# Running sums of the forget gate in four one-pass products, and eight transfers moved from SyncE to GpSimd

## Chip, core and metric

The kernel runs on one core of one Trainium2 chip. The metric is the device time of one execution in microseconds (us). Before the change the median of three runs is 347.56 us (347.39 to 348.7).

## What is computed

One decoder block over 256 tokens (`S`) of width 1024 (`D`), in float32. The reference, cut to what matters here:

```python
h = rms_norm(x, attn_norm_g)
proj = h @ w_in              # qa, ka, va, qb, kb, vb, f_logit, g_logit
...                          # branch a: attention over qa, ka, va with rotary embedding
log_f = log_sigmoid(f_logit + b_forget)          # 8 heads
c = cumsum(log_f, axis=-1)                       # branch b, the forgetting attention
s = (qb . kb) * scale + c[t] - c[s]              # causal, then softmax, then times vb
gates = sigmoid(g_logit + b_gate)                # 2 branches x 1024
merged = gates[0] * (o_a @ w_branch_moba) + gates[1] * (o_b @ w_branch_fox)
x = x + merged @ w_out
h2 = rms_norm(x, ffn_norm_g)
u, g = split(h2 @ w_ffn_up)                      # 2 x 2816
x = x + (silu(causal_conv3(g)) * u) @ w_ffn_down
```

## The kernel before

Every large product is made of float32r products, which TensorE takes in one pass. Each operand is split into a high part (the value written as float32r) and a low part (the rest), and three products are added in PSUM: high times high, high times low, low times high. Small products stay in plain float32: the transposes, the products of the forget gate and some of the scores.

The weights come in chunks of 128 x 2048 float32 (1 MB). SyncE issues them in order through `load` (L131) into three buffers `raw`. For each half of a chunk ScalarE writes the high part `whi` (L134) and VectorE the low part `wlo` (L135). `use` takes a half and loads ahead by five halves (`AHEAD`). The first chunk of weights comes together with x, transposed, in eight transfers of 384 KB (`lead`, L95). `split_x` (L162, L164, L165) makes the high and low parts of x times the norm's gain, and L102 and L103 split the weights beside it.

TensorE's order is written out by hand in the text of the kernel. The other engines and the DMA issues are ordered by a scheduler at build time, which places an instruction where it finds the engine free and the operands and buffers ready. An instruction can so stand far ahead of its place in the text. An engine then works off its own list strictly in order.

The stages, in TensorE's order: nine warm-up products on a constant (L171); the projections qa, ka, va, qb, kb (`project`, L247); the running sums (`forget_c`, L364); three pairs of heads of branch a's scores (`scores`, L400, L407); vb and the gate projections (`gate`, L247) with the rest of the attention between them (L413, L450, L464); the branch products (L604); the output projection and the up projection (`rows_of`, L653, L654) with the down projection (L792) in between; the final sums and stores (L815, L816, L825, L826).

What the change touches:

- `forget_a` to `forget_c`: the logits are made in `forget_products` (L326), turned to tokens by heads in `forget_b`, and sent through the log-sigmoid in small VectorE and ScalarE steps that end in `lf`, 128 x 16 (L356). In `forget_c` two plain float32 products (L364), one per half of the tokens, multiply `lf` with the triangle `tri` (128 x 128, a slice of the constants `cst`). VectorE copies the sums to SBUF (L366) and adds the first half's last column to the second half (L367), ScalarE's queue writes them to DRAM (L369) and reads them back spread over 128 partitions (L370). They are used in the scores of branch b.
- `norm1`: the sum of squares (L222 transposes, L224 sums) and the inverse root (L200 to L205).
- `ones`, a 128 x 128 block of ones as float32r (L638), used in `norm2_sum` (L719).
- `gate_bias` (L477): two calls, two transfers of 256 KB in each, g = 0 and 1 and later g = 2 and 3, into the two buffers `lows`. The third waits until `gate` has used the first (L490), the fourth until it has used the second. They are consumed by L490.
- `start_turn` (L298): turns of the queries and keys by 16 small transfers each, half of them issued by GpSimd and half by SyncE; `end_turn` (L304) copies them out on ScalarE, and for branch b `halve` (L392, L393) splits them.
- `spread_x` (L738): 16 transfers of 64 KB that lay the residual out for the final sums. GpSimd issues 11 and SyncE five. They wait for `turn_x` (L733), and are read at L805 and L815.

Of the kernel before, what the change touches and what calls it, by code (L numbers as in the profile page):

```python
# [8 lines left out]
F32 = mybir.dt.float32  # L9
F32R = mybir.dt.float32r  # L10
BF16 = mybir.dt.bfloat16
AF = mybir.ActivationFunctionType
ALU = mybir.AluOpType
# [4 lines left out]
P = 128  # L18
S = 256
NT = 2  # L20
# [3 lines left out]
NH = 8  # L24
# [18 lines left out]
def decoder_block(ctx, tc, a, out):  # L43
    nc = tc.nc
# [6 lines left out]
    def T(shape, tag, bufs=1, dt=F32):  # L51
        return sb.tile(shape, dt, tag=tag, bufs=bufs, name=tag)

    def bank():
        return ps.tile([P, 512], F32, tag="bank", bufs=8, name="bank")
# [97 lines left out]
    def col(c, n=1):  # L153
        return sm[:, c:c + n]
# [32 lines left out]
    cst = T([P, 832], "cst")  # L187
    nc.sync.dma_start(cst, a["consts"])
    ident = cst[:, 0:128]
    tri = cst[:, 128:256]  # L190
    mask3 = cst[:, 384:768]
    cos2 = cst[:, 768:832].rearrange("p (t c) -> p t c", t=NT)
    wfr = T([P, KT, NH], "wfr")
# [2 lines left out]
    def rsqrt_mean(dst, ss, n, shape, tag, bufs=2):  # L196

        w = T([P, 3] + shape, tag, bufs)
        v, y, t = w[:, 0], w[:, 1], w[:, 2]
        nc.vector.tensor_scalar(v, ss, 1.0 / n, EPS, op0=ALU.mult, op1=ALU.add)  # L200
        nc.scalar.activation(t, v, AF.Ln)
        nc.scalar.activation(y, t, AF.Exp, scale=-0.5)
        nc.vector.scalar_tensor_tensor(t, v, -0.5, y, op0=ALU.mult, op1=ALU.mult)
        nc.vector.tensor_tensor(t, t, y, op=ALU.mult)
        nc.vector.scalar_tensor_tensor(dst, t, 1.5, y, op0=ALU.add, op1=ALU.mult)  # L205
# [13 lines left out]
    def norm1():  # L219
        ssp = bank()  # L220
        for t in range(NT):
            nc.tensor.transpose(ssp[:, t * P:(t + 1) * P], xss[:, 0, t * P:(t + 1) * P], ident)  # L222
        ss = T([P, NT], "ss1")
        nc.vector.tensor_reduce(ss, ssp[:, 0:S].rearrange("p (t c) -> p t c", t=NT), axis=AX.X, op=ALU.add)  # L224
        rsqrt_mean(rs, ss, D, [NT], "rsv")

        for i in range(2):
            gr = sm[:, C_GR + 16 * i:C_GR + 16 * (i + 1)][:, None, :].to_broadcast([P, NT, 16])
            rc = T([P, NT, 16], f"rc{i}")
            rsn = T([P, NT, 16], f"rsn{i}")  # L230
            nc.vector.tensor_tensor(rc, cos2[:, :, 0:16], gr, op=ALU.mult)
            nc.vector.tensor_tensor(rsn, cos2[:, :, 16:32], gr, op=ALU.mult)
            rope.append((rc, rsn))
# [76 lines left out]
    bias = T([P, NH, 384], "bias")  # L310

    fg = {}

    def forget_a():
        wf4 = T([P, KT, 32], "wf4")
        nc.gpsimd.memset(wf4, 0.0)
        nc.gpsimd.tensor_tensor(wf4[:, :, 0:8], wfr, g1[:, :, None].to_broadcast([P, KT, NH]), op=ALU.mult)
        fg["wf4"] = wf4
# [12 lines left out]
    def forget_b():  # L331
        fs = fg["fs"]
        ft = bank()
        for t in range(NT):
            nc.tensor.transpose(ft[:, t * P:(t + 1) * P], fs[:, t * P:(t + 1) * P], ident)
        z = T([P, NT, NH], "z")
        nc.vector.tensor_reduce(z, ft[:, 0:S].rearrange("p (t g e) -> p t g e", t=NT, e=32)[:, :, :, 0:NH].rearrange("p t g h -> p t h g"), axis=AX.X, op=ALU.add)
        for t in range(NT):
            nc.vector.scalar_tensor_tensor(z[:, t], z[:, t], rs[:, t:t + 1], col(C_BF, NH), op0=ALU.mult, op1=ALU.add)

        az = T([P, NT, NH], "az")
        nc.scalar.activation(az, z, AF.Abs)
        e = T([P, NT, NH], "ez")
        nc.scalar.activation(e, az, AF.Exp, scale=-1.0)
        u = T([P, NT, NH], "uz")
        nc.vector.tensor_scalar_add(u, e, 1.0)
        l = T([P, NT, NH], "lz")
        nc.scalar.activation(l, u, AF.Ln)
        d = T([P, NT, NH], "dz")
        nc.vector.scalar_tensor_tensor(d, u, -1.0, e, op0=ALU.add, op1=ALU.subtract)  # L350
        r = T([P, NT, NH], "rz")
        nc.vector.reciprocal(r, u)
        nc.vector.tensor_tensor(d, d, r, op=ALU.mult)
        nc.vector.tensor_tensor(l, l, d, op=ALU.subtract)
        lf = T([P, NT, NH], "lf")
        nc.vector.scalar_tensor_tensor(lf, z, 0.0, l, op0=ALU.min, op1=ALU.subtract)  # L356
        fg["lf"] = lf

    def forget_c():
        lf = fg["lf"]  # L360
        cp = bank()
        c0, c1 = (cp[:NH, t * P:(t + 1) * P] for t in range(NT))
        for t, c in enumerate((c0, c1)):
            nc.tensor.matmul(c, lf[:, t], tri, start=True, stop=True)  # L364
        cT = T([P, 2, 384], "pT", 4)[:NH, 0, 0:S]
        nc.vector.tensor_copy(cT, cp[:NH, 0:S])  # L366
        nc.vector.tensor_scalar_add(cT[:, P:S], cT[:, P:S], cT[:, P - 1:P])  # L367
        cd = dr.tile([NH, S], F32, name="cd")
        nc.scalar.dma_start(cd, cT)  # L369
        nc.scalar.dma_start(bias[:, :, P:P + S], bass.AP(tensor=cd.tensor, offset=cd.offset, ap=[[0, P], [S, NH], [1, S]]))  # L370
# [101 lines left out]
    bg = []  # L472

    def gate_bias():
        for g in range(len(bg), len(bg) + 2):
            bg.append(T([P, 2, S], "lows", 2).rearrange("p j t -> p (j t)"))
            nc.sync.dma_start(bg[g], a["bg"][:, g])  # L477

    def gate(c, late=False):
        g, h = divmod(c, 2)  # L480
# [23 lines left out]
    project(0, pq, 1)  # L504
    project(1, pk, 0)
    norm1()
    forget_products()
    q0 = start_turn(finish_qk(pq, 0, 0), 0)
# [6 lines left out]
    project(3, pq, 0)  # L515
    project(3, pq, 1, (0,))
    forget_b()
    project(3, pq, 1, (1,))
    q1 = finish_qk(pq, 1, 0)
    pk = banks()  # L520
    project(4, pk, 0)
    gate_bias()
    end_turn(q0, 0, 0)
    end_turn(k0, 0, 1)
    project(4, pk, 1, (0,))
    state["hold"] = True
    project(4, pk, 1, (1,))
    forget_c()
    scores(0, 0)
    state["hold"], state["behind"] = False, (None, last_max[0])  # L530
# [38 lines left out]
    values(0, (0, 1))  # L569
    values(0, (2, 3))  # L570
    gate_bias()
    for c in (4, 5, 6):
        gate(c)
# [60 lines left out]
    hx = T([P, KT, 2, 2, P], "pp", 1, F32R)  # L634
    acc = [[None, None] for _ in range(NT)]
    rs2 = T([P, S], "rsB")
    ones = T([P, P], "ones", 1, F32R)
    nc.scalar.activation(ones, cst[:, 256:384], AF.Copy)  # L638

    def place(t, dh):  # L640
# [88 lines left out]
    x1 = lt[:, :, S:2 * S]  # L729
    turned_x = lt[:, :, 2 * S:3 * S]  # L730
# [4 lines left out]
    def spread_x():  # L735
        for r in range(4):
            for b in range(4):
                (nc.sync if b == 3 or r == b == 0 else nc.gpsimd).dma_start(x1[32 * b:32 * (b + 1), r::4], turned_x[32 * r:32 * (r + 1), b::4])  # L738


    acts = {}
# [94 lines left out]
    for f in range(NF):  # L836
        low = up_finish(f, first[f] if f < 2 else up_products(f))
        if f % 2 == 0 and f >= 4:
            down(f // 2 - 2)
        if TURN <= f < TURN + KT:  # L840
            turn_x(f - TURN, low)
        if f == TURN + KT:
            spread_x()
# [73 lines left out]
```

## Time and profile before

| | before |
|---|---|
| median of 3 runs (range) | 347.56 us (347.39 to 348.7) |
| the profiled execution's own time | 347.68 us |
| its span, first to last instruction | 345.9 us |
| TensorE (PE) busy | 341.7 us |
| VectorE (DVE) busy | 296.4 us |
| ScalarE (ACT) busy | 220.5 us |
| GpSimd (POOL) busy | 24.2 us |
| read from and written to HBM | 67.64 MB and 1.06 MB |

The profiled execution lies 0.12 us above the median of the runs, and its time 1.78 us above its span. The parts of a profile used here: the busy times of the engines; the waits, which name for an engine's idle time what ended it; the chain of work that ended last, followed back from the last instruction; the timeline, which lists instructions by start time with neighbours of one kind merged (start, us from the first start to the last end, engine, line, operation, output and inputs, count); and windows, which give busy time by stretch of the span with the DMA engines' mean busy share and rate. PE is the matrix product, PEld the loading of its stationary operand, SPq, ACTq and POOLq are the sequencers that issue transfers.

### The profile page before, as it was taken

What the parts mean: (1) busy time and instruction counts of PE and PEld (TensorE: products, weight loads), DVE (VectorE), ACT (ScalarE), POOL (GpSimd) and SP (SyncE); (2) the same over time, 40 slices, a digit from 0 to 9 for tenths busy, and PEclk for the clock granted to TensorE, in tenths of its full rate; (3) what the DMA queues carried; (4) which work ended last, traced back from release to release, by engine and by line L of the source; (5) the groups of instructions that cost most, each with busy time, mean ns of one, the idle gap of its engine ahead of it and who ended that gap; (6) DMA issues with size and microseconds to landing.
All of it is one profiled execution on the core that took longest, in us unless ns stands there. A gap on an engine that the chain in (4) does not pass through costs nothing.

```text
span 345.9 us, 5459 instructions
## 1 busy us (share of the span) xinstructions
PE 341.7 (99%) x1983; PEld 299.9 (87%) x1983; DVE 296.4 (86%) x562; ACT 220.5 (64%) x384; POOL 24.2 (7%) x51
## 2 busy tenths in 40 slices
PE   9999999999999999999999999999999999999996
PEld 5888888888888888889999998989898999989885
DVE  4899997999989578997999998897859898968853
ACT  4968556877599485745767876664645674756430
POOL 0000261044000000000000000000000000060000
PEclk9999999999999999999999999999999999999999
DMA  7987859667941827484726645664573565594003
GB/s 268 409 345 261 305 173 308 243 181 216 353 166 36 331 85 245 158 312 173 244 81 284 208 169 233 243 244 142 222 244 121 200 214 196 186 282 142 2 0 121
DMA packets 17466, 72.19 MB, mean 209 GB/s; under 512 B 2856, under 2 KB 7408, under 8 KB 10016
## 3 DMA queue, kind: packets, MB, share of 16 engines
q1 hardware_dynamic: 14864, 69.02, 55.8%
q0 software_dynamic: 1376, 1.77, 2.1%
q10 hardware_dynamic: 1200, 1.06, 0.9%
q8 instruction: 15, 0.25, 0.3%
q14 instruction: 11, 0.09, 0.1%
HBM read 67.64 MB, written 1.06 MB: 199 GB/s over the span
## 4 chain that ended last, share of the span: by engine, by line
PE 99%; DVE 0%; issue 0%
PE bank L247 30%; PE bank L653 26%; PE bank L792 17%; PE bank L654 13%; PE bank L604 6%; PE bank L464 2%; PE bank L171 1%; PE bank L450 1%; PE bank L400 1%; PE bank L407 1%; PE bank L413 0%; PE bank L618 0%; PE bank L326 0%; PE bank L364 0%; DVE s L825 0%; PE bank L719 0%
## 5 line engine op out<-in xcount | busy, mean ns | idle before, releaser
L135 DVE TENSOR_TENSOR wlo<-raw,whi 128x1024 fp32r<-128x1024 f32 x94 | 113.8, 1218 | 5.5 <-ACT whi L134 5.2
L134 ACT ACTIVATE whi<-raw 128x1024 fp32r<-128x1024 f32 x94 | 97.9, 1052 | 18.4 <-PE bank L247 5.9
L247 PE MATMUL bank<-whi,x 128*128 128x512 f32 x320 | 84.3, 383 | 0.1
L653 PE MATMUL bank<-pp,whi 128*128 128x512 f32 x232 | 76.6, 382 | 0.0
L247 PEld LDWEIGHTS bank<-whi,x 128*128 128x128 f32 x320 | 60.3, 190 | 10.8 <-ACT whi L102 1.2
L654 PE MATMUL bank<-pp,wlo 128*128 128x256 f32 x232 | 63.2, 273 | 0.0
L653 PEld LDWEIGHTS bank<-pp,whi 128*128 128x128 f32 x232 | 43.8, 189 | 6.1
L247 PE MATMUL bank<-wlo,x 128*128 128x512 f32 x160 | 47.6, 379 | 0.0
L654 PEld LDWEIGHTS bank<-pp,wlo 128*128 128x128 f32 x232 | 44.5, 192 | 0.2
L247 PEld LDWEIGHTS bank<-wlo,x 128*128 128x128 f32 x160 | 30.2, 189 | 4.3
L792 PE MATMUL bank<-whi,qT 128*128 128x512 f32 (+1 forms) x92 | 27.8, 370 | 0.0
L761 DVE TENSOR_TENSOR sq<-bank,lows 128x256 f32<-128x256 f32 x44 | 18.2, 416 | 8.7 <-ACT lows L760 8.6
L766 ACT ACTIVATE s<-sq,sm 128x256 f32<-128x256 f32 x22 | 13.1, 598 | 18.8 <-DVE sq L762 18.8
L738 POOL DMA_DIRECT2D lead<-lead x11 | 5.8, 536 | 219.4 <-DVE lead L733 219.3
L298 POOL DMA_DIRECT2D pp<-pp x32 | 17.1, 542 | 46.8 <-DVE qf L268 22.1
L769 ACT ACTIVATE s<-s 128x256 f32<-128x256 f32 x22 | 9.1, 415 | 16.4 <-DVE s L768 16.4
L792 PEld LDWEIGHTS bank<-whi,qT 128*128 128x128 f32 x92 | 17.2, 189 | 2.3
L653 PE MATMUL bank<-pp,bias 128*128 128x512 f32 x56 | 18.7, 382 | 0.0
L760 ACT ACTIVATE lows<-bank 128x256 f32<-128x256 f32 x44 | 15.8, 369 | 2.8 <-PE bank L654 2.7
L792 PE MATMUL bank<-wlo,qT 128*128 128x512 f32 (+1 forms) x46 | 17.0, 370 | 0.0
L604 PE MATMUL bank<-whi,pp 128*128 128x512 f32 x64 | 16.9, 382 | 0.0
L431 ACT ACTIVATE s<-s,nm 128x128 f32<-128x128 f32 (+1 forms) x32 | 14.1, 448 | 2.8 <-DVE nm L428 2.8
(181 smaller groups left out, 592.2 us busy)
## 6 DMA issues: line engine op xcount, KB each, us to landing
raw<-in_wu SPq DMA_DIRECT2D x22, 1024.0 KB, 4.9
raw<-in_wd SPq DMA_DIRECT2D x11, 1024.0 KB, 4.9
raw<-in_qkv SPq DMA_DIRECT2D x9, 1024.0 KB, 5.5
raw<-in_wg SPq DMA_DIRECT2D x8, 1024.0 KB, 5.5
raw<-in_wb SPq DMA_DIRECT2D x4, 1024.0 KB, 4.9
raw<-in_wo SPq DMA_DIRECT2D x4, 1024.0 KB, 4.7
lead<-in_lead SPq DMA_DIRECT2D x8, 384.0 KB, 6.5
raw<-in_qkv SPq DMA_DIRECT2D x2, 512.0 KB, 8.4
```

The lines of the kernel that those rows point to most:

```text
L134: whi = nc.scalar.activation(hi, raw, AF.Copy)
L135: wlo = nc.vector.tensor_tensor(lo, raw, hi.bitcast(F32), op=ALU.subtract)
L247: nc.tensor.matmul(pt[t], lhs[:, k, t * P:(t + 1) * P], rhs, start=(k == 0 and i == 0), stop=(k == KT - 1 and i == 2))
L298: queues[r % len(queues)].dma_start(raw[32 * r:32 * (r + 1), :, b], y[32 * b:32 * (b + 1), r])
L431: last_exp[:] = [nc.scalar.activation(s[:, j, c], s[:, j, c], AF.Exp, scale=-1.0, bias=nm[:, j, i:i + 1], accum_out=l[:, j, i:i + 1])]
L604: nc.tensor.matmul(ps_[t], lhs[:, t * P:(t + 1) * P], rhs, start=(k == 0 and i == 0), stop=(k == 3 and i == 2))
L653: nc.tensor.matmul(two[i], wh[:, c], both, start=(k == 0), stop=False)
L654: nc.tensor.matmul(two[i][:, 0:S], wl[:, c], high, start=False, stop=(k == KT - 1))
L760: nc.scalar.activation(lows[:, i:i + 1].rearrange("p b (a t) -> p b a t", a=2), apart(two[i][:, S:2 * S], 1), AF.Copy)
L761: nc.vector.tensor_tensor(halves(ev[:, i:i + 1]), apart(two[i][:, 0:S], 1), halves(lows[:, i:i + 1]), op=ALU.add)
L766: nc.scalar.activation(cv, g, AF.Identity, scale=col(C_CW + 2 * NF + f), bias=col(C_CB + f))
L792: nc.tensor.matmul(o, lhs, rhs, start=(first and i == 0), stop=(end and i == 2))
```

## The change

The log gates `lf` are copied to a high part as float32r and the rest is kept as a low part, both in a new tile `lf2`. The triangle is converted once to a float32r tile `tri` by ScalarE in `norm1`, written between L224 and the inverse root. In `forget_c` four float32r products (two parts, two halves of the tokens) take the place of two float32 products. `ones` takes over the buffer of `tri`. Of the four transfers of `gate_bias`, all but the first are issued by GpSimd, and all 16 of `spread_x` are.

```diff
-    tri = cst[:, 128:256]
...
         nc.vector.tensor_reduce(ss, ssp[:, 0:S].rearrange("p (t c) -> p t c", t=NT), axis=AX.X, op=ALU.add)
+        nc.scalar.activation(tri, cst[:, 128:256], AF.Copy)
         rsqrt_mean(rs, ss, D, [NT], "rsv")
...
     fg = {}
+    tri = T([P, P], "tri", 1, F32R)
...
         nc.vector.scalar_tensor_tensor(lf, z, 0.0, l, op0=ALU.min, op1=ALU.subtract)
-        fg["lf"] = lf
+        lf2 = T([P, 4, NT, NH], "lf2", 1, F32R)
+        nc.vector.tensor_copy(lf2[:, 0], lf)
+        nc.vector.tensor_tensor(lf2[:, 1], lf, lf2[:, 0].bitcast(F32), op=ALU.subtract)
+        fg["lf"] = lf2
...
         for t, c in enumerate((c0, c1)):
-            nc.tensor.matmul(c, lf[:, t], tri, start=True, stop=True)
+            for l in range(2):
+                nc.tensor.matmul(c, lf[:, l, t], tri, start=(l == 0), stop=(l == 1))
...
             bg.append(T([P, 2, S], "lows", 2).rearrange("p j t -> p (j t)"))
-            nc.sync.dma_start(bg[g], a["bg"][:, g])
+            (nc.gpsimd if g else nc.sync).dma_start(bg[g], a["bg"][:, g])
...
-    ones = T([P, P], "ones", 1, F32R)
+    ones = T([P, P], "tri", 1, F32R)
...
-                (nc.sync if b == 3 or r == b == 0 else nc.gpsimd).dma_start(x1[32 * b:32 * (b + 1), r::4], turned_x[32 * r:32 * (r + 1), b::4])
+                nc.gpsimd.dma_start(x1[32 * b:32 * (b + 1), r::4], turned_x[32 * r:32 * (r + 1), b::4])
```

## The prediction

> **What bounds the kernel now.** I read the busy times first, then what TensorE waited for, then the chain that ended last.
>
> ```profile
> span 345.9 us, 5459 instructions
> PE 341.7 (99%) x1983; PEld 299.9 (87%) x1983; DVE 296.4 (86%) x562; ACT 220.5 (64%) x384; POOL 24.2 (7%) x51
> PE 99%; DVE 0%; issue 0%
> PE bank L171 <- PEq L910: 0.8, 1, 0.8
> ```
>
> The first two lines are the page's span and busy times, the third is the head of its chain, the fourth is the whole answer for PE's waits. PE waits for no other engine and no transfer in the profile; the chain is PE alone. Because matmul ends are modelled, I check that with starts. Pieces of the chain (start, us, what):
>
> ```profile
> 4.64 4.60 PE bank L247 x18
> 9.28 11.92 PE bank L247 x54
> ...
> 79.14 15.74 PE bank L247 x72
> ...
> 342.62 0.42 DVE s L825
> ```
>
> In mid-kernel 72 products of 512 columns take 15.74 us, 0.219 us each. The 54 from 9.28 on take 0.221 each: PE runs at its pace there too. The 18 before them take 4.60 us where 3.93 would do: 0.67 us are lost while the first weights come in. After 9.28 there is no slack to win but in the products themselves, until the last VectorE step at 342.62 and the final store. What the change can do is therefore: shorten PE's own work, or delay PE where it now has no wait.
>
> **The change, part by part.**
>
> *The four products.* PE's timeline around the two of before, and around the nearest one-pass pair, L719:
>
> ```profile
> 58.50 0.59 PE L247 MATMUL bank<-whi,x 128*128 128x512 f32 x2
> 59.03 0.60 PE L364 MATMUL bank<-cst,lf 128*8 128x128 f32 x4
> 59.56 0.38 PE L400 MATMUL bank<-kT,qT 64*128 64x128 f32 x2
> ...
> 177.58 0.27 PE L654 MATMUL bank<-pp,wlo 128*128 128x256 f32 x1
> 177.69 0.41 PE L719 MATMUL bank<-lows,ones 128*128 128x256 f32 x2
> 177.94 0.38 PE L653 MATMUL bank<-pp,whi 128*128 128x512 f32 x1
> ```
>
> The last two L247 start at 58.50 and end, by 0.219 each, at 58.94. L364 starts at 59.03 and L400 at 59.56, so the two float32 products (four records) hold PE for 0.62 us, 0.09 of it before them. No one-pass product of 128 columns is in the trace. Going by columns from L654 (0.11 us for 256 columns) four would take 0.22 us, the low end, a saving of 0.40. The high end is that each costs as much as one float32 product of the same shape, 0.53 / 2 = 0.265: 1.06 us and the 0.09, a loss of 0.53. I take the L719 pair, 0.25 us for 512 columns with two weight loads, and keep the 0.09 for the turn to the float32 L400: 0.34, a saving of 0.28 us. The Trainium skill (TensorE: Matmul & The Clock Gate, "Back-to-back issue gap") gives about 81 ns for one 128-column product in a stream with weight loads, so an estimate of 0.32 us for four and a saving of 0.30 or less; its gap formula gives 109 ns at 256 columns, which the 0.11 us of L654 agrees with, but no run here shows 128 columns.
>
> *Two VectorE steps and one of ScalarE.* VectorE's and ScalarE's timelines:
>
> ```profile
> 55.45 0.17 DVE L356 SCALAR_TENSOR_TENSOR lf<-z,lz 128x16 f32<-128x16 f32 x1
> 55.54 0.36 DVE L268 TENSOR_SCALAR qf<-qf,rs 128x8 f32<-128x8 f32 x2
> 55.80 1.28 DVE L269 TENSOR_TENSOR qn<-bank,qf 128x512 f32<-128x512 f32 x2
> 57.00 1.22 DVE L135 TENSOR_TENSOR wlo<-raw,whi 128x1024 fp32r<-128x1024 f32 x1
> 59.67 0.41 DVE L366 COPY pT<-bank 8x256 f32<-8x256 f32 x1 [1.45 <-PE bank L364]
> ...
> 19.60 0.29 ACT L638 ACTIVATE ones<-cst 128x128 fp32r<-128x128 f32 x1
> 22.59 0.20 ACT L201 ACTIVATE rsv<-rsv 128x2 f32<-128x2 f32 x1 [2.71 <-DVE rsv L200]
> ```
>
> The copy to `lf2` and the subtraction are the size of L356: 2 x 0.17 = 0.34 us. VectorE idles 1.45 us just behind, waiting for L364, and takes them up. Right behind L356 they are done at 56.0; even behind the L135 that starts at 57.00 they end at 57.00 + 1.22 + 0.34 = 58.56, before PE needs them at 58.94. If that cover were gone (one more split of 1.22 ahead of them) PE would wait 0.8 us, 0.2%; the splits behind them feed halves that PE comes to several halves later (`AHEAD`). The new conversion of the triangle is the instruction `ones` is now, the same 128 x 128: it can take its place at 19.60, ahead of 2.71 us of idle time. `ones` in turn can come only after L364 and is needed at 177.69; ScalarE is idle a third of the span. Nothing for these.
>
> *Five issues of the spread.* GpSimd's, SyncE's and VectorE's timelines:
>
> ```profile
> 302.51 5.99 POOL L738 DMA_DIRECT2D lead<-lead  x11 [219.25 <-DVE lead L733]
> ...
> 302.01 3.29 SPq L738 DMA_DIRECT2D lead<-lead  x5
> ...
> 329.83 0.69 DVE L805 TENSOR_TENSOR s<-bank,lead 128x512 f32<-128x512 f32 x1
> ...
> lead<-lead POOLq DMA_DIRECT2D x11, 64.0 KB, 3.7
> ```
>
> GpSimd issues 16 instead of 11: 5.99 / 11 x 16 = 8.7 us, until 311.2, and the last lands 3.7 us later, at 314.9 (the fence's last line is the DMA page's median to landing). L805 reads the result first, at 329.83: 15 us of cover, and nothing else is queued on GpSimd. A tile late beyond that would hold VectorE at L805, and then the end one for one. On SyncE the two loads behind come up to 3.3 us sooner if a buffer `raw` is free; PE does not wait for them, so no gain.
>
> *Three transfers of the gate bias.*
>
> SyncE's and GpSimd's timelines, the page's row of these transfers (KB, us to landing), and the line that reads them:
>
> ```profile
> 33.94 0.42 SPq L477 DMA_DIRECT2D lows<-in_bg  x1
> ...
> 37.97 0.42 SPq L477 DMA_DIRECT2D lows<-in_bg  x1
> ...
> 89.77 0.33 SPq L477 DMA_DIRECT2D lows<-in_bg  x1
> ...
> 18.73 0.67 POOL L317 TENSOR_TENSOR wf<-wfr,g 128x64 f32<-128x64 f32 x1 [17.54 <-DMA wfr<-in_wf]
> ...
> lows<-in_bg SPq DMA_DIRECT2D x4, 256.0 KB, 4.8
> L490 DVE SCALAR_TENSOR_TENSOR lead<-bank,rs,lows x8: 741/747/750, 88.3 to 122.5; 128x512 f32<-128x512 f32 x8
> ```
>
> The third and fourth wait for a buffer as before, have GpSimd to themselves after its turns, and land some 5 us after; of the eight reads by L490, the last four, at most 122.5, are theirs, each behind a gate's products. The loads behind them on SyncE are freed of their wait; PE did not wait for those. Nothing for these two. The issue itself is unknown on GpSimd at 256 KB: between the 0.54 us of a 64 KB one (5.99 / 11) and four times that, 2.2; either is idle time there.
>
> The second (g = 1) is another matter. Its buffer is fresh and it waits for nothing. On SyncE it stood behind the weights; GpSimd is idle for 17.54 us, from 1.2 to 18.73. `ones`, written hundreds of lines later, stands at 19.60 on ScalarE: whatever is ready is put forward into idle time. So I expect this transfer at about 1.3 us, in the middle of the first weights:
>
> ```profile
> 2.00:10.00 8.00, 7.89 (x28) 5.08 (x27) 5.37 (x12) 3.71 (x8) 0.00 (x0) 1.00 0.98 353
> ...
> 6.31 0.63 ACT L102 ACTIVATE whi<-lead 128x512 fp32r<-128x512 f32 x1 [0.80 <-DMA lead<-in_lead]
> 8.20 0.51 ACT L164 ACTIVATE x<-lead,g 128x256 fp32r<-128x256 f32 x1 [1.26 <-DMA lead<-in_lead]
> 8.61 0.61 ACT L102 ACTIVATE whi<-lead 128x512 fp32r<-128x512 f32 x1
> ```
>
> From 2 to 10 us the DMA engines are busy 0.98 of the time and move 353 GB/s (the window's last columns); ScalarE waits 1.26 us for a `lead`, splits it by 9.22, and PE goes on at 9.28. 0.262 MB more at 353 GB/s are 0.74 us, by which that lead, and with it all of PE's chain, comes later. The ends: nothing, if it lands after the leads or in idle time; 0.74 and no more, as it cannot take more than its own bytes. The Trainium skill (DMA: Bandwidth & Descriptors, "Issuing engines are not separate DMA queues") says that transfers started by GpSimd run on the same 16 DMA engines and interleave with the others; by that rule the loss is real whenever the issue is early, and the 0.98 above shows that nothing was free.
>
> **Sum**, against the profiled execution's 347.68 us: -0.28 (products) + 0.74 (early transfer) = 348.14. The median of the runs is 0.12 lower than that execution, so 348.0 us. A measurement of this kernel can tell about 0.5%, 1.7 us, from no change; this is 0.1%.
>
> **Rivals.**
>
> 1. *The early transfer costs nothing*, because the scheduler keeps it near 34 us or it slips between the leads. That SyncE's first two were put forward no further than 34 and 38 us speaks for it; GpSimd's 17.54 us of idle time against. 347.68 - 0.28 - 0.12 = 347.3 us.
> 2. *The products stay slow*: one-pass products of 128 columns run like the float32 ones. No row of fewer than 256 columns speaks against it. With the early transfer, 347.56 + 0.53 + 0.74 = 348.8; without it 348.1.
> 3. *Slower: GpSimd's queue is blocked at the keys of branch b.* The third bias transfer must wait for L490, and GpSimd works in order. If the scheduler put it ahead of the eight issues of the last turn (79.04), those would wait.
>
> ```profile
> 79.04 4.22 POOL L298 DMA_DIRECT2D pp<-pp  x8 [2.09 <-ACT pT L440]
> ...
> 90.02 1.13 ACT L304 ACTIVATE kT<-pp,sm 128x1024 f32<-128x1024 f32 x1
> 91.19 1.06 ACT L392 ACTIVATE qn<-kT 128x1024 fp32r<-128x1024 f32 x1
> ...
> 92.52 1.22 DVE L393 TENSOR_TENSOR qn<-kT,qn 128x1024 fp32r<-128x1024 f32 x1
> ...
> 96.03 0.36 PE L413 MATMUL bank<-qn 64*128 64x256 f32 x1
> ```
>
> From the first issue to split keys it takes 4.22 + 3.7 (landing, by the spread's) + 1.13 + 1.06 + 1.22 = 11.3 us, and PE uses them at 96.03: the point that decides is an issue later than 84.7. Behind the bias at 89.77 they start near 90.3, and PE waits until 101.6: 5.6 us, 347.56 - 0.28 + 5.6 = 352.9. Against it: the buffer comes free ten us after the turn's issues are ready, so an order by readiness puts the turn first.
>
> Faster by 0.5% would need 1.74 us; PE idles 4.2 us in the whole span, none of which an edit here touches.
>
> **How the numbers follow.** The early transfer 0.45, rival 1 0.36, rival 2 0.07, rival 3 0.05; 0.07 for what I don't see, most of it another order of VectorE or ScalarE that makes PE wait (0.03 slower, 0.02 same, 0.02 faster). Within 0.5% lie the first three and 0.02: 0.90; slower 0.08, faster 0.02. The likeliest gives 348.0. The range runs from the lowest run less the largest saving, 347.39 - 0.40, rounded down to 346.9, to the dearest case of rival 2, 348.8, and 0.2 for the scatter of runs: 349.0.
>
> **What would show it.** L364: four records, and from the end of the last L247 to the start of L400 0.34 us instead of 0.62; if above 1 us, rival 2. GpSimd's timeline: an L477 near 1.3 us, and in PE's chain the piece from 4.64 that lasts 5.3 instead of 4.60; if it stands near 34 us and PE's pieces keep their starts until 59, rival 1. L738: 16 on GpSimd until about 311, L805 where it was. PE's waits: still the one line; any other line there, at L364 or L413 above all, makes the prediction wrong.

## The result, and the profile after

| | before | after |
|---|---|---|
| median (range) | 347.49 us (347.37 to 348.7) | 350.33 us (349.19 to 351.45) |
| ratio, 95% interval | | 1.0074 [1.0049, 1.0099] |
| the profiled execution's time, span | 347.68, 345.9 us | 349.19, 347.4 us |

The change made the kernel slower, by 2.84 us. The prediction, 348.0 (346.9 to 349.0), was wrong: it forecast a loss of 0.1%, and the loss is 0.74%, beyond its range. The profiled execution after the change is the shortest of its six runs (349.19), so its rows show the smaller part of the loss; two more profiles stand under e14_after_again. Here and below ratios leave out disturbed runs, of which the experiments had two, of 359.25 us (e1_products) and 398.52 us (e4_swapped). In the changed kernel the lines behind the edits have numbers higher by up to five: the keys' copy is still L304, but L364 is now L369, L400 is L405, L450 is L455, L477 is L482, L490 is L495, L738 is L743 and L805 is L810.

The page after: span, busy times, and the head of the chain that ended last.

```profile
span 347.4 us, 5454 instructions
...
PE 341.8 (98%) x1983; PEld 300.5 (87%) x1983; DVE 297.2 (86%) x564; ACT 222.3 (64%) x385; POOL 28.5 (8%) x59
...
PE 76%; DVE 12%; DMA 5%; ACT 3%; issue 3%; POOL 1%; SPq 0%; ACTq 0%; DVEq 0%
```

And PE's waits (us in total, times, longest):

```profile
PE bank L405 <- ACT kT L304: 0.9, 1, 0.9
PE bank L171 <- PEq L915: 0.8, 1, 0.8
PE bank L405 <- DVE lead L495: 0.5, 1, 0.5
```

PE's busy time is unchanged, and the chain, which was 99% PE, now runs through VectorE, the transfers and ScalarE. Two waits are new, both at the scores products: one on the keys (`kT`), one on the gate's VectorE step that must empty PSUM banks. Together they are 1.4 us, and the span is 1.5 us longer. From the first product with `V` (L464 before at 98.27, L469 after at 99.76) to the last VectorE step (342.62 and 344.12) both profiles take 244.35 us, to 0.01: the whole loss of this execution lies ahead of 100 us. PE's timeline at the first wait, after:

```profile
58.63 0.59 PE L247 MATMUL bank<-whi,x 128*128 128x512 f32 x2
59.06 0.41 PE L369 MATMUL bank<-tri,lf 128*8 128x128 f32 x4
60.38 0.49 PE L405 MATMUL bank<-kT,qT 64*128 64x128 f32 x4 [0.91 <-ACT kT L304]
```

The four products start when PE comes to them, and then PE has no keys. Why the keys are late is in SyncE's list, here before:

```profile
47.45 0.53 SPq L131 DMA_DIRECT2D raw<-in_qkv  x1
48.31 5.24 SPq L298 DMA_DIRECT2D pp<-pp  x8
53.65 4.93 SPq L131 DMA_DIRECT2D raw<-in_wg  x3
```

and after:

```profile
46.77 0.53 SPq L131 DMA_DIRECT2D raw<-in_qkv  x1
47.40 0.38 SPq L131 DMA_DIRECT2D raw<-in_wg  x1
48.03 8.43 SPq L298 DMA_DIRECT2D pp<-pp  x8
56.59 1.52 SPq L131 DMA_DIRECT2D raw<-in_wg  x2
```

The eight L298 are SyncE's half of the keys' turn. Before, all three loads of gate weights stand behind it. After, the scheduler has put the first, 1 MB, ahead of it. (A 1 MB load of `in_qkv` goes out just ahead in both kernels, so after the change there are two.) No edit names either: SyncE's list came out in another order because other instructions of it were gone. The small issues then take 8.43 us instead of 5.24, and the pieces of the turn land later. The transfers issued from 47 to 60 us (count, KB each, median us to landing), before and after:

```profile
pp<-pp SPq DMA_DIRECT2D x9, 32.0 KB, 4.6
pp<-pp POOLq DMA_DIRECT2D x8, 32.0 KB, 4.6
```

```profile
pp<-pp SPq DMA_DIRECT2D x8, 32.0 KB, 7.0
pp<-pp POOLq DMA_DIRECT2D x8, 32.0 KB, 6.5
```

GpSimd's half is late too, though nothing was put ahead of it on GpSimd. ScalarE's timeline shows what follows, before and then after:

```profile
57.24 1.16 ACT L304 ACTIVATE kT<-pp,sm 128x1024 f32<-128x1024 f32 x1 [2.11 <-DMA pp<-pp]
58.68 1.06 ACT L134 ACTIVATE whi<-raw 128x1024 fp32r<-128x1024 f32 x1 [0.29 <-DMA raw<-in_wg]
59.65 1.25 ACT L261 ACTIVATE sq<-bank,rs 128x512 f32<-128x512 f32 x2
```

```profile
59.17 1.15 ACT L304 ACTIVATE kT<-pp,sm 128x1024 f32<-128x1024 f32 x1 [4.04 <-DMA pp<-pp]
60.23 1.04 ACT L134 ACTIVATE whi<-raw 128x1024 fp32r<-128x1024 f32 x1
61.17 1.25 ACT L261 ACTIVATE sq<-bank,rs 128x512 f32<-128x512 f32 x2
```

Before, the keys' copy ended at 58.40, 1.16 us ahead of L400 at 59.56. That margin is gone: the copy starts 1.93 us later. Behind it in ScalarE's list stand `whi` and the squares `sq`, which are 1.5 us later as well, and VectorE, which goes on from `sq`, passes it on to the gate step, whose first half frees the banks for the scores. VectorE's and PE's timelines at the gate step, before:

```profile
94.79 1.41 DVE L490 SCALAR_TENSOR_TENSOR lead<-bank,rs,lows 128x512 f32<-128x512 f32 x2
...
94.81 0.97 PE L450 MATMUL bank<-cst,s 64*128 64x64 f32 x24
```

and after:

```profile
96.67 1.40 DVE L495 SCALAR_TENSOR_TENSOR lead<-bank,rs,lows 128x512 f32<-128x512 f32 x2
...
95.77 0.96 PE L455 MATMUL bank<-cst,s 64*128 64x64 f32 x24
...
97.46 0.49 PE L405 MATMUL bank<-kT,qT 64*128 64x128 f32 x4 [0.46 <-DVE lead L495]
```

The gate step and the PE work beside it started together before; now the gate step is 0.90 behind, and PE waits 0.46 for the banks, the second new line. In two other profiles below the step is 0.70 and 1.43 behind and PE waits 0.26 and 0.98 (e2_bias, e12_kept_margin), each time 0.44 to 0.45 less than the lag. Before, the step was 0.02 ahead, so the room was some 0.46 us, an estimate from these rows. From the first scores product to the first with `V` PE takes 38.71 us before (59.56 to 98.27) and 39.38 after (60.38 to 99.76): 0.67 more, for a wait of 0.46 with a slower order of the products around it. The other steps of the change are on GpSimd's timeline after:

```profile
18.37 0.67 POOL L318 TENSOR_TENSOR wf<-wfr,g 128x64 f32<-128x64 f32 x1 [17.18 <-DMA wfr<-in_wf]
18.98 0.72 POOL L482 DMA_DIRECT2D lows<-in_bg  x1
...
311.29 1.60 POOL L743 DMA_DIRECT2D lead<-lead  x3 [0.90 <-issue]
```

The transfer g = 1 stands at 18.98 (L482), not at 1.3; the spread is issued by 312.9.

### The profile page after: what moved, and what is told of

It is laid out like the page before. It is cut to its first block, busy times and chain, and to the rows that moved or that the text cites. A ratio compares the mean times of both kernels' runs of the same rounds, so it can differ in the third digit from the quotient of the medians.

```text
span 347.4 us, 5454 instructions
## 1 busy us (share of the span) xinstructions
PE 341.8 (98%) x1983; PEld 300.5 (87%) x1983; DVE 297.2 (86%) x564; ACT 222.3 (64%) x385; POOL 28.5 (8%) x59
## 3 DMA queue, kind: packets, MB, share of 16 engines
q10 hardware_dynamic: 1200, 1.06, 1.0%
HBM read 67.64 MB, written 1.06 MB: 198 GB/s over the span
## 4 chain that ended last, share of the span: by engine, by line
PE 76%; DVE 12%; DMA 5%; ACT 3%; issue 3%; POOL 1%; SPq 0%; ACTq 0%; DVEq 0%
PE bank L658 26%; PE bank L797 16%; PE bank L659 13%; PE bank L247 11%; PE bank L609 6%; DVE wlo L135 5%; DMA raw<-in_wg 2%; PE bank L469 2%; ACT whi L134 1%; DMA pp<-pp 1%; DMA lead<-in_lead 1%; DVE ss L262 1%; DVE s L433 1%; DVE bias L381 1%; POOL pp L298 1%
## 5 line engine op out<-in xcount | busy, mean ns | idle before, releaser
L247 PE MATMUL bank<-whi,x 128*128 128x512 f32 x320 | 84.5, 384 | 0.1
L247 PEld LDWEIGHTS bank<-whi,x 128*128 128x128 f32 x320 | 60.5, 191 | 10.4 <-issue 0.9
L247 PE MATMUL bank<-wlo,x 128*128 128x512 f32 x160 | 47.6, 379 | 0.0
L247 PEld LDWEIGHTS bank<-wlo,x 128*128 128x128 f32 x160 | 30.4, 190 | 4.4
L743 POOL DMA_DIRECT2D lead<-lead x16 | 8.5, 537 | 205.5 <-PE bank L659 202.2
L298 POOL DMA_DIRECT2D pp<-pp x32 | 16.9, 535 | 48.6 <-ACT whi L134 24.2
L771 ACT ACTIVATE s<-sq,sm 128x256 f32<-128x256 f32 x22 | 13.1, 595 | 11.5 <-DVE sq L767 11.5
```

The costliest lines, as they stand in the source:

```text
L247: nc.tensor.matmul(pt[t], lhs[:, k, t * P:(t + 1) * P], rhs, start=(k == 0 and i == 0), stop=(k == KT - 1 and i == 2))
L298: queues[r % len(queues)].dma_start(raw[32 * r:32 * (r + 1), :, b], y[32 * b:32 * (b + 1), r])
L771: nc.scalar.activation(cv, g, AF.Identity, scale=col(C_CW + 2 * NF + f), bias=col(C_CB + f))
```

## The experiments

The theory tested: with g = 1 off SyncE the first gate load passes the keys' turn; that costs the margin of the keys' copy, and through ScalarE's order that of the gate step. Rivals: the four products cost time, or the moved issues themselves do. `after(a, b)` puts a behind b in the order of one engine; `state["k0"]` is SyncE's last issue of the keys' turn (in `e4_swapped` and `e5_half` all eight). Medians of the kernel before, beside these runs, are 347.76 (first four), 347.83 (next four), 347.90 (next four) and 347.61 us (last three).

**e1_products.** The kernel before with the products alone:

```diff
+            for l in range(2):
+                nc.tensor.matmul(c, lf[:, l, t], tri, start=(l == 0), stop=(l == 1))
...
```

> Only the forget gate's products are changed; all transfers are issued as before. Theory A (one weight load of 1 MB passes the SyncE half of the keys' turn, the keys land late and TensorE waits at the first scores): that order is the old one here, so nothing is late, and the products save 0.2 to 0.3 us: 347.2 us, ratio 0.999, no wait at L405. Rival B (the new parts of the products, or the later `ones`, delay VectorE and ScalarE): about 350 us, with a wait at L405 or later.

Measured: 347.91 us, ratio 1.0002 [0.9992, 1.0012], for 347.2 expected; profiled 347.22, span 345.4, no new wait, products to scores 0.34 us. The products don't cause the loss. Nor does their saving show in the median, though the profile has it.

**e2_bias.** The bias moves alone:

```diff
-            nc.sync.dma_start(bg[g], a["bg"][:, g])
+            (nc.gpsimd if g else nc.sync).dma_start(bg[g], a["bg"][:, g])
```

> Only the gate bias is moved (three transfers to GpSimd); products and spread as before. Theory A: the weight load passes the keys' turn as in the changed kernel, so 350 to 350.6 us, ratio 1.007 to 1.009, and TensorE waits about 0.9 us for the keys at L400 and again some 0.5 us near 97 us. Rival B: 347.5 us, no wait.

Measured: 349.78 us, 1.0062 [1.0040, 1.0084]. It is a little under the range expected. SyncE's order is that of after (the load at 47.01, the turn 47.86 and 7.90 long). PE's waits at the scores:

```profile
PE bank L400 <- ACT kT L304: 0.6, 1, 0.6
PE bank L400 <- DVE lead L490: 0.3, 1, 0.3
```

Moving the three transfers by itself makes most of the loss.

**e3_kept.** The whole change, with the load held behind the turn:

```diff
+                    ld = nc.sync.dma_start(raw[:, j * w:(j + 1) * w], src[:, j * w:(j + 1) * w])
+                    if c == ("wg", 0):
+                        after(ld, state["k0"])
```

> The whole change, with one edge that keeps the first gate load (raw<-in_wg) behind the SyncE half of the keys' turn, as it stood before. Theory A: TensorE's waits vanish and the time is 347.2 us, ratio 0.999; granted clock 1.0 in all runs. Rival C (the gate bias or the spread issued by GpSimd costs by itself, through the DMA engines or GpSimd's queue): stays at 349 to 350.5 us.

Measured: 348.16 us, 1.0017 [1.0005, 1.0029], not the 347.2 expected. Neither wait is in PE's list, and PE goes from the products to the scores at once:

```profile
59.06 0.41 PE L371 MATMUL bank<-tri,lf 128*8 128x128 f32 x4
59.39 0.49 PE L407 MATMUL bank<-kT,qT 64*128 64x128 f32 x4
```

One edge in SyncE's order takes back some three quarters of the loss, with all eight transfers still on GpSimd.

**e4_swapped.** The kernel before, without the change, with the order turned round:

```diff
+                    if c == ("wg", 0):
+                        for t in state["k0"]:
+                            after(t, ld)
```

> The kernel before, nothing of the change in it, but with the first gate load put ahead of the SyncE half of the keys' turn. Theory A: the loss appears without the change: 349.5 to 350.6 us, ratio 1.006 to 1.009, keys land at 8 us instead of 5, TensorE waits near 60 us. Rivals B and C: 347.5 us.

Measured: 348.98 us, 1.0037 [1.0020, 1.0054]: the loss comes without the change, but smaller than expected. At the scores PE waits on the keys only:

```profile
PE bank L405 <- ACT kT L309: 1.1, 1, 1.1
```

There is no line for the gate step. ScalarE's timeline has the reason:

```profile
56.34 1.06 ACT L137 ACTIVATE whi<-raw 128x1024 fp32r<-128x1024 f32 x1 [1.53 <-PE bank L250]
59.30 1.15 ACT L309 ACTIVATE kT<-pp,sm 128x1024 f32<-128x1024 f32 x1 [1.90 <-DMA pp<-pp]
60.36 1.25 ACT L264 ACTIVATE sq<-bank,rs 128x512 f32<-128x512 f32 x2
```

Here a `whi` stands ahead of the late copy, and `sq` comes at 60.36, not at 61.17. That gave e9_whi_first.

**e5_half.** As e4_swapped, with only the first 512 KB of the load ahead of the turn (`after(*((t, ld) if j == 0 else (ld, t)))`):

> The kernel before, with the first gate load cut in two and only the first half (512 KB) put ahead of the SyncE half of the keys' turn, the second half behind it. Theory A (the turn's small transfers queue behind the load's bytes): the copy of the keys starts about 1 us later than the 57.24 us of before, inside the 1.1 us that it has to spare, so TensorE waits 0 to 0.3 us: 347.6 to 348.1 us, ratio 1.000 to 1.001. Rival E (any load in that place costs, by order and not by bytes): as with the whole load, 349.0 us, ratio 1.004.

Measured: 348.53 us, 1.0032 [1.0020, 1.0045]; waits of 0.4 on the keys and 0.3 on the gate step. Theory A's time missed: by the time, half the bytes can't be told from all of them, and rival E stays open. The turn's issues still take 7.55 us, and the copy starts at 58.95. But the turn itself started later here (48.93). Counted from its first issue on SyncE, the copy starts 10.02 us behind, between the 7.4 to 9.2 of the eight profiles with the turn first and the 10.6 to 11.5 of the seven with the whole load ahead on SyncE. That speaks for the bytes; one profile does not settle it.

**e6_spread.** The spread moved alone (`nc.gpsimd.dma_start(x1[...` for all 16):

> Only the spread's five issues move from SyncE to GpSimd. The result is read at 329.83 us and lands near 316: theory A and my sum: no change, 347.8 us, ratio 1.000, TensorE without a wait. Rival C: 348.2 us or more, and a wait near the down products.

Measured: 348.32 us, 1.0010 [1.0000, 1.0019]; the span of the profiled run is 345.8 us. The time lies in rival C's range, but without the wait that rival C names, and without the two waits at the scores. Of the 0.1%, about half is time outside the span (1.9 to 2.0 us for 1.8).

**e7_bias_kept.** The bias moves of e2_bias with the edge of e3_kept:

> Only the gate bias is moved to GpSimd, with the first gate load kept behind the SyncE half of the keys' turn. Theory A: 347.8 us, ratio 1.000, against 349.8 without the edge. Rival C (GpSimd-issued bias transfers cost by themselves): 348.5 us or more; the load alone put ahead gave 349.0, which leaves 0.8 us open that this run gives to one or the other.

Measured: 348.25 us, 1.0014 [1.0002, 1.0027], and no new wait in PE's list. The time lies between the two expectations. Against 1.0062 without the edge, the order causes most of the loss, not the issuing engine of the bias; a cost of some 0.1% of the moved issues is not ruled out.

**e8_g1_back.** The whole change, with g = 1 on SyncE again (`nc.gpsimd if g > 1 else nc.sync`):

> The whole change, but g = 1 of the gate bias issued by SyncE again; g = 2 and 3 and the whole spread stay on GpSimd. Theory A: the one transfer was what kept the order; it is the old one here, so 347.5 to 348.0 us, ratio 0.999 to 1.001, against 350.3 for the whole change. Rival C: 348.2 us or more.

Measured: 348.48 us, 1.0027 [1.0013, 1.0041]. That is above theory A's range, and in rival C's. The scheduler puts the turn (48.43) ahead of the load (54.56) again, and the keys' wait is gone. At the scores one line stays:

```profile
PE bank L405 <- DVE lead L495: 0.5, 1, 0.5
```

So one transfer's place decides SyncE's order. The gate step's room can go without the first loss: PE comes to the scores 0.29 us earlier (59.27), and here `whi`, with `sq` behind it, waits for a load (the copy at 57.61, `whi` at 59.68, `sq` at 60.65). By starts this profile takes 39.95 us from scores to `V` (59.27 to 99.22), 1.24 more than before, of which the line explains 0.46. Where the rest goes stays open, and so does whether the excess over theory A is rival C's or comes of late work on VectorE and ScalarE.

**e9_whi_first.** After, with one edge on ScalarE:

```diff
+            if c == ("wg", 0) and h == 0:
+                after(state["copy", 0, 1], whi)
```

> The whole change, with one edge: ScalarE turns the first half of the first gate load (whi) ahead of its copy of the keys, as it did of itself in the kernel whose only edit is the load put ahead of the turn. SyncE's order and the late landing stay as after the change. Theory (two margins: keys' copy late, then the gate step late because whi and the square wait behind the keys' copy on ScalarE): the first wait (scores product on the keys, 0.9 us of rows after the change) stays, the square starts about 0.8 us earlier (60.4 for 61.2), and the second wait (scores' banks on the gate step, 0.5 us) goes or falls to 0.1: the last forget-to-value interval as in that kernel, 38.7 us for 39.4, and 349.2 to 349.8 us, ratio 1.004 to 1.006. Rival (the second wait comes of PE's own order and not of ScalarE's): it stays, and the time is that after the change, 350.3, ratio 1.007.

Measured: 349.07 us, 1.0047 [1.0024, 1.0069], 0.13 below the range expected. The keys' wait stays, but is 1.7 for the 0.9 expected, the gate step's is gone, and the interval from scores to `V` is 38.70 us (61.81 to 100.51), as expected. `sq` starts at 61.66, not at the 60.4 expected, as the whole turn came later here; against the scores it starts 0.15 ahead, where it was 0.79 behind (60.38 and 61.17 after the change). VectorE's and PE's timelines show the gate step beside PE's work again:

```profile
97.16 1.41 DVE L498 SCALAR_TENSOR_TENSOR lead<-bank,rs,lows 128x512 f32<-128x512 f32 x2
...
97.06 0.97 PE L458 MATMUL bank<-cst,s 64*128 64x64 f32 x24
```

That PE came later is not the reason: with keys' waits of 1.7 and 1.8 the gate step's wait is still there in e14_after_again and e15_after_look. So the second loss comes of ScalarE's order behind the late copy. By the profiles it is 0.67 us; the time's intervals alone wouldn't tell 1.0047 from 1.0074.

**e10_after_margin.** After, with two of VectorE's copies on ScalarE:

```diff
-    state["behind"] = turn(0, 0), turn(0, 1, nc.vector.tensor_copy)
+    turn(0, 0)
+    state["behind"] = turn(0, 1), None
```

> The whole change, but the two copies of the turn's second half go to ScalarE in place of VectorE, so that VectorE has about 1 us less to do ahead of the gate step. Nothing on SyncE changes. Theory: the keys still come late (wait of about 0.9 us), the gate step's first half comes 0.7 to 1 us earlier and the second wait (0.5 us) is gone: 349.3 to 349.8 us, ratio 1.004 to 1.006. Rival (ScalarE, not VectorE, holds the gate step, and has no room): ScalarE's two more copies put the square or the later keys off, and it is 350.3 or above.

Measured: 349.75 us, 1.0060 [1.0042, 1.0078]: inside the range, the gate step's wait gone, the keys' wait 1.9 for the 0.9 expected. The windows of this profile (us, busy times and counts of PE, PEld, DVE, ACT and POOL, PE's granted clock, DMA share, GB/s) show one thing more:

```profile
60.00:61.00 1.00, 0.00 (x0) 0.00 (x0) 0.00 (x0) 1.00 (x2) 0.00 (x0) 1.00 1.02 434
...
62.00:63.00 1.00, 1.00 (x12) 0.84 (x10) 1.00 (x7) 1.00 (x3) 0.00 (x0) 0.54 0.93 393
...
65.00:66.00 1.00, 1.00 (x5) 0.82 (x5) 0.22 (x2) 1.00 (x6) 0.00 (x0) 0.76 0.58 182
```

A microsecond after the wait of 1.88 us the granted clock falls to half; it is 0.50 in the two windows left out between 63 and 65. At 0.50 while it lasts, that is 0.92 + 2 + 0.48 = 3.4 us, in which 1.7 us of PE's work are lost. It is the longest run of this kernel, 350.96. PE's lost work gives the gate step time, so this profile does not show that the copies removed the wait; in e12_kept_margin, with the same copies and the clock at 1.00, it is there.

**e11_margin.** The products alone, with the copies of e10_after_margin:

> The products alone, with the turn's second half copied by ScalarE as in the run before: more room at both places. Theory: no wait of PE on the keys' copy or the gate step; the saving of the products (0.28 us of PE) reaches the end: 347.2 to 347.6 us, ratio 0.999. Rival (ScalarE's copies in place of VectorE's hold up something else, or the saving is given back at another wait as the products alone showed 1.000): 347.8 to 348.3, ratio 1.000 to 1.0015.

Measured: 347.59 us, 0.9993 [0.9979, 1.0007], no new wait. It is the lowest median of the altered kernels, in the range expected, but the interval holds 1: not shown to beat it.

**e12_kept_margin.** The whole change, with e3_kept's edge and the same copies:

> The whole change with SyncE's order kept (the first gate load behind the keys' turn) and the turn's second half copied by ScalarE. Theory (the loss is the two waits, nothing of the eight moved issues themselves): 347.3 to 347.8 us, ratio 0.9985 to 1.000. Rival (the moved issues have a cost of their own, which the kept order alone left at 1.0017): 348.1 to 348.4, ratio 1.0015 again. Second rival (the small rest of 1.0017 was the thin margin at the gate step, missed in some runs): equal to the products with the same copies, within 0.1 us.

Measured: 348.31 us, 1.0017 [1.0003, 1.0032]. The time lies in the first rival's range, but the profile has a wait that none of the three foresaw, large enough for it, so the run decides nothing on a cost of the moved issues:

```profile
PE bank L407 <- DVE lead L497: 1.0, 1, 1.0
```

VectorE's timeline says who is late now:

```profile
91.77 1.22 DVE L137 TENSOR_TENSOR wlo<-raw,whi 128x1024 fp32r<-128x1024 f32 x1 [0.98 <-ACT whi L136]
```

ScalarE's `whi` comes late, and VectorE, with room of its own, waits 0.98 us for it ahead of the gate step. ScalarE's own list shows that it had waited 3.24 us for a load (`in_wg`) just before, so the two copies more are not shown to be the reason; with them and the old order, e11_margin has no such wait of PE.

**e13_load_on_act.** After, the load issued by ScalarE:

```diff
+                    (nc.scalar if c == ("wg", 0) else nc.sync).dma_start(raw[:, j * w:(j + 1) * w], src[:, j * w:(j + 1) * w])
```

> The whole change, with the first gate load issued by ScalarE's queue in place of SyncE's; it is still ahead of the keys' turn in time. It tells by what the load holds the turn up. Theory Q (the eight small issues of SyncE stand behind the load's bytes in SyncE's own queue): SyncE's eight issues take 5 to 5.5 us again (8.43 after the change, 5.24 before), the keys' copy starts near 57 and PE does not wait for it: 347.8 to 348.6 us, ratio 1.000 to 1.002. Theory B (the load's 1 MB shares the same DMA engines, whoever issues it): the pieces of both queues land as late as after the change (about 6.5 us, longest above 8), the keys' copy starts at 58.5 to 60 and PE waits 0.5 to 1.5 us: 349 to 350.3, ratio 1.004 to 1.007.

Measured: 352.37 us, 1.0129 [1.0111, 1.0146]. The load did not stay ahead of the turn: ScalarE issued it 0.68 us behind SyncE's first piece. The lists of SyncE and ScalarE:

```profile
48.10 6.53 SPq L298 DMA_DIRECT2D pp<-pp  x8
...
48.78 0.34 ACTq L131 DMA_DIRECT2D raw<-in_wg  x1
```

The pieces of the turn, with the load in a third queue:

```profile
pp<-pp SPq DMA_DIRECT2D x9, 32.0 KB, 7.0
pp<-pp POOLq DMA_DIRECT2D x8, 32.0 KB, 7.2
```

They land as late as after the change, and the copy starts at 60.20: theory B, the shared DMA engines. The place in SyncE's queue adds to the issuing time (6.53 us here, 8.43 after), but the pieces land late without it. The Trainium skill says so (DMA: Bandwidth & Descriptors, "Issuing engines are not separate DMA queues": transfers run on the same 16 engines and interleave whichever engine starts them), and the landings agree. The time was missed by 2 us. The copy came 0.2 us later than expected at most, but the scheduler put other work behind it on ScalarE, and PE waited elsewhere:

```profile
PE bank L369 <- DVE lf L359: 2.7, 1, 2.7
PE bank L405 <- DVE pT L371: 1.0, 1, 1.0
```

On VectorE the high and low parts of the log gates stood behind a step that needs one of ScalarE's (L201, at 61.25, right behind the copy).

**e14_after_again, e15_after_look.** The kernel after, unaltered, two more profiles:

> The kernel after the change, unaltered, for a second profile and its spread beside the others. Theory (the wait for the keys depends on when the turn's last piece lands beside the load, 0.6 to 1.9 us in the profiles with this order so far, and a long wait is followed at times by some 4 us of TensorE at half its clock, worth 1.6 us): the first wait differs from the 0.91 us of the first profile; runs lie from 349.2 to 351.5, median 349.6 to 350.5, and those with the granted clock at 0.996 or less are the longest, by 1 us or more. Rival (the loss is the same in every run): all within 0.5 us of 349.2, or of 350.3, whatever their clock.

> The kernel after the change once more, for a third profile. Theory: waits of PE on the keys' copy and on the gate step again, the first between 0.6 and 1.9 us, the second near 0.5 us; if the first is above 1.8 us the granted clock falls to about 0.5 for some 4 us behind it. Rival: 0.9 and 0.5 us to 0.1.

Measured: 349.87 us, 1.0065 [1.0049, 1.0081], and 349.67. The keys' waits of the two:

```profile
PE bank L405 <- ACT kT L304: 1.7, 1, 1.7
```

```profile
PE bank L405 <- ACT kT L304: 1.8, 1, 1.8
```

The gate step's is 0.5 in both. The first profile, with 0.9, was of the shortest run. By starts, the scores come 2.08 and 2.17 us behind the products (0.53 before), so 1.55 and 1.64 are lost at the keys and 0.68 at the gate step, 2.2 to 2.3 of the 2.26 us between the medians. The clock did not fall in these (0.999 and above), though runs went up to 350.76, so not every long run is the clock's. But in the first six runs after the change, in e2_bias and in e9_whi_first the one run with a mean clock under 0.996 is the longest (351.45, 351.6 and 351.85 us), and in e10_after_margin the two such runs are the two longest (350.96 and 350.49). For those the theory fits.

## Why the prediction was wrong

- *The four products, -0.28.* Right. Where PE doesn't wait they start 0.33 to 0.34 us ahead of the scores (e3_kept, e1_products), as predicted from L719. The 0.09 us ahead of the products is gone, and PE goes from the last pair of L247 to the scores in 0.77 us in both, 1.06 before: 0.29 saved. Rival 2 is out. The 81 ns of the Trainium skill (TensorE: Matmul & The Clock Gate, "Back-to-back issue gap"), an estimate of 0.32 for four, agree. But e1_products gained nothing that its median shows, and e11_margin 0.07% with an interval over 1: the saving shows in PE's time alone.
- *VectorE's and ScalarE's small steps, 0.* Right: VectorE made the parts at 55.04 and 55.25, done 3.6 us before PE came.
- *The spread, 0.* No wait came of it: L810 read at 328.76, the issues ended at 312.9, predicted 311.2, and landed within 6.2 us at most, so by about 319. Alone it measured 1.0010 (e6_spread), half of which stays unexplained.
- *The early transfer, +0.74.* Wrong. It stood at 18.98, behind L318, and PE's first pieces kept their length. That was the outcome of rival 1 (chance 0.36), though at neither of the places it named. With no transfer among the first weights, no run here tests the price of 0.74, or the rule cited beside it. Without the term the sum gives 347.3, further from the measured time: the 0.74 brought the forecast nearer by luck, by a loss that did not happen.
- *"The loads behind them on SyncE are freed of their wait; PE did not wait for those. Nothing for these two."* This reasoning is the step that failed. It stands there for g = 2 and 3; the g = 1 paragraph after it does not look at SyncE at all, and g = 1 is the one that counts (e8_g1_back). I asked what the transfers meet on GpSimd and whether PE waits for the loads, not what the freed loads run into on SyncE, so the sum has no term for it. Taking g = 1 off SyncE put 1 MB ahead of the keys' turn, which cost 2.2 to 2.3 us by the two later profiles: 1.55 to 1.64 at the keys and 0.68 at the gate step. e8_g1_back, e3_kept and e7_bias_kept take the order away, and with it the keys' wait; e4_swapped brings the keys' wait about by itself. The numbers to see it by were in the profile of before: 1.16 us between the keys' copy and L400. The room at the gate step, some 0.46 us, needed other profiles to be read.
- *Rival 3* had the right mechanism, keys held up by a transfer of another kind ahead of them, on the wrong queue and at the wrong keys: branch a's, by SyncE. The prediction gave "another order of VectorE or ScalarE that makes PE wait" 0.03 for slower; orders that shift when an instruction is taken from a list deserved far more.
- *What would show it.* The last sign came: a second line in PE's waits.

Open: why e3_kept, e6_spread and e7_bias_kept stay 0.10 to 0.17% above before with neither wait in PE's lists. Some 0.2 us of e6's and e7's is outside the span. In e3's and e7's profiles scores to `V` takes 38.88 and 38.85 us (38.71 before), and weight loads of the scores (PEld) wait 0.3 and 0.2 us for the gate step, so part of it is the same thin room. A cost of the moved issues themselves, of 0.1 to 0.2%, is not ruled out. Why single runs of the changed kernel differ by over a microsecond is open too, beyond the few in which the clock fell.

## What to carry to other kernels

Taking an instruction off a queue moves everything behind it: list what the queue holds next, what each of those competes with when it comes earlier, and how much time its consumers have to spare. Read that spare time from the start of the first use less the end of the last producer, for each handover within the next tens of microseconds; here it was 1.2 and some 0.5 us, and a wait list without entries said nothing of it. An order that matters should be fixed with an edge: one edge (e3_kept) took the ratio from 1.007 to 1.002.

## What the hardware showed that was not expected

- One more 1 MB load started within a microsecond of 16 transfers of 32 KB put their median landing from 3.6 to 5.0 us (eight profiles without) to 6.2 to 7.6 us (eight with). It did so whether SyncE issued the load just ahead or ScalarE just behind the first piece, and for the pieces issued by GpSimd as well as SyncE's. The issues of eight small ones in the load's own queue went from 5.1 to 6.0 us to 7.9 to 8.9 us, and took 6.53 with the load in ScalarE's (e13_load_on_act).
- TensorE's granted clock fell to 0.50 for some 3.4 us after one idle wait of 1.88 us (e10_after_margin), in which about 1.7 us of PE's work were lost; not after waits of 1.69 (e9_whi_first), 1.68 and 1.77 (e14_after_again, e15_after_look), nor after the 2.70 us of e13_load_on_act's profile. The mean clock of that profiled run is 0.995. Single runs without a profile show as low a mean (0.993 to 0.995) in one run each of after, e2_bias and e9_whi_first, another of e10_after_margin and three of the five of e13_load_on_act; in the kernels with the turn first all runs in the ratios are at 0.998 or more. So the same kernel shows a fall in some executions only, and it is not always seen in the time: the three of e13_load_on_act are within 0.2 us of its profiled run at 1.000. The Trainium skill (TensorE: Matmul & The Clock Gate, "Part 1: The HAM clock gate") gives half clock as the idle state, which agrees, after an idle window of about 3.4 us, and full clock again after as long a busy one. The 3.4 us of the lapse agree with the second; the first does not hold here, where the clock fell after an idle wait of 1.88 us.
